# A state-space stage's W2 operand: transposed per batch on TensorE, or multiplied on VectorE from factors that were transposed once

## The chip, the cores and the metric

The kernel runs on one core of a Trainium2 chip. The metric is the device time of one execution in microseconds, the median of several runs. The engines are named as in the profile: PE is TensorE, PEld its weight load, DVE is VectorE, ACT is ScalarE, POOL is GpSimd, SP is SyncE, whose queue issues the DMAs. "L689" is line 689 of the kernel before; the changed kernel has other line numbers.

## The reference

A two-layer encoder trunk over 1024 frames of 1024 channels. Layer 0 projects its normalised input to `u`, gates, `q`, `k`, `v`; a diagonal complex state-space model works on `u` (64 groups of 16 channels, 64 states each), retention works on `q, k, v`; both are gated and projected back. Layer 1 is a gated convolution module. What matters here is the state-space model:

```python
lb = exp(a * dt)                          # complex, one per group g and state n
bb = ((lb - 1) / a)[..., None] * b        # complex, g x n x h (16 channels)
s[t] = lb * s[t - 1] + einsum('gnh,gh->gn', bb, u[t])
y[t] = real(einsum('ghn,gn->gh', c, s[t])) + d * u[t]
...
y = gelu(y); y = y * sigmoid(y @ glu_w + glu_b)
y_s5 = y * silu(g_s5)
```

The kernel takes eight frames at a time: the input of such a block to the state is a product with the table `W2[(j, h), n] = lb^j[n] * bb[n, h]`, j = 0 to 7.

## The kernel before, in words

Large products are made of three matmuls on a high and a low part of each operand (L146, L147, L148, 128x512). The front of layer 0 (`layer0_front`) first makes eight blocks of `u` (`u_block`), each stored to DRAM, and, between them, the parameters of the state-space model (`s5_params`): the powers of `lb` in `self.pr`, `self.pi` (state on the partitions) and the factors `bb` in `self.bbr`, `self.bbi`. GpSimd makes the latter last.

Then come 16 gate blocks (`gate_block`), two for each of eight batches B of the state-space model; a batch is eight groups. Each gate block is two halves of 24 matmuls in a PSUM tile `mm_g`, scaled on VectorE (L329) and sent through a SiLU on ScalarE (L330). Between the matmuls of the gate blocks stands the work of the batches:

- `s5_tables(B)`: GpSimd makes tables of 128x512 by outer products (`outer`, L642 to L644): Mr and Mi (powers times `bb`, state on the partitions), the rotations Tc and Ts, and W3. They have 18 instructions a batch in a fixed chain. ScalarE makes R8 (L671). The tables of batch B + 1 are made while batch B runs; Mr and Mi have one buffer and are freed by kp (below).
- `s5_states(B)`: loads U; PE transposes Mr and Mi, four 128x128 each (L689), ScalarE copies the results from PSUM to W2r and W2i (L691). PE multiplies W2 with U into the PSUM tiles V (L700). VectorE rotates V (L708 to L713), scans it (L715), rotates back (L722 to L725) and writes S (L726 to L728). PE also multiplies C with Mr and Mi to kp (L734, L735); ScalarE copies it to Kg, VectorE adds the diagonal (L738), PE transposes it (kt, L740), and it goes through DRAM (`k_d`, L744, L747) to become W1 (L749).
- `s5_out(B - 1)`: y = W1 x U + W3 x S on PE (L764, L770), copied by ScalarE, stored.

The order on each engine is decided when the kernel is built: a scheduler places the instructions by due times of its own, and each engine and SP's queue then run theirs strictly in that order. Tiles come from pools with a number of buffers per tag; a tile that takes a buffer waits until the last reader of the earlier one is done. PSUM has three banks for the gate blocks and five for everything else in this stage. After batch 7 the retention follows, then the rest of layer 0 and layer 1.

Of the kernel before, what the change touches and what calls it, by code (L numbers as in the profile page):

```python
# [11 lines left out]
F32 = mybir.dt.float32  # L12
# [3 lines left out]
ALU = mybir.AluOpType  # L16
# [3 lines left out]
P = 128  # L20
# [19 lines left out]
class Trunk:  # L40
# [167 lines left out]
    def layer0_front(self, st):  # L208
        tc, nc, A = self.tc, self.nc, self.A
# [30 lines left out]
        for kb in range(KB):  # L240
# [6 lines left out]
            t = xt[kb] = ev.tile([P, T], F32, name=f"x_{kb}", tag="xin", bufs=8)  # L247
            g = self.vec(V_NG0, kb)
            for h in range(2):
                c = slice(h * HALF, (h + 1) * HALF)  # L250
# [58 lines left out]
        def u_block(nb):  # L309
            ut = uv.tile([P, 8, P], F32, name=f"ut_{nb}", tag="ut", bufs=2)  # L310

            def evac(h, ps):
                r = self.R[:, h * HALF:(h + 1) * HALF]
                self.u_evac[nb] = nc.vector.tensor_tensor(
                    ut[:, ::-1, h * 64:(h + 1) * 64], ps[:].rearrange("p (m j) -> p j m", j=8),
                    r.rearrange("p (m j) -> p j m", j=8), op=ALU.mult)
            if nb < 2:
                for h in range(2):
                    evac(h, u01[nb][h])
            else:  # L320
                scaled(nb, self.wnext(f"u{nb}"), f"u{nb}", evac)
            nc.sync.dma_start(self.u_d[nb].rearrange("j h g m -> (h g) j m"), ut[:])
# [24 lines left out]
        for nb in range(5, 8):  # L347
            u_block(nb)
        self.s5_tab, self.s5_back, self.s5_last = {}, {}, None
        self.s5_tables(0)  # L350
        for nb in range(8, 24):
            B = (nb - 8) // 2
# [284 lines left out]
    def outer(self, B, o_r, o_i, ar, ai, br, bi, view, op_r=ALU.subtract, op_i=ALU.add):  # L637

        gp = self.nc.gpsimd
        for o, op, (a0, b0), (a1, b1) in ((o_r, op_r, (ar, br), (ai, bi)), (o_i, op_i, (ar, bi), (ai, br))):  # L640
# [2 lines left out]
            yield gp.tensor_tensor(view(o), a0, b0, op=ALU.mult)  # L643
            yield gp.tensor_tensor(o, o, t[:], op=op)  # L644

    def s5_tables(self, B):


        nc, w = self.nc, self.s5
        gp, v = nc.gpsimd, nc.vector  # L650
        qs = slice(4 * B, 4 * B + 4)

        Mr, Mi = self.big(f"Mr_{B}", "Mr", 1), self.big(f"Mi_{B}", "Mi", 1)
        vm = lambda ap: ap.rearrange("p q (j h) -> p q j h", j=8)
        bj = lambda t: t[:, qs, :].unsqueeze(2).broadcast_to([P, 4, 8, 16])
        pj = lambda t, o=0: t[:, o:o + 8, qs].rearrange("p j q -> p q j").unsqueeze(3).broadcast_to([P, 4, 8, 16])
        made = [self.outer(B, Mr[:], Mi[:], bj(self.bbr), bj(self.bbi), pj(self.pr), pj(self.pi), vm)]

        Tc, Ts = self.big(f"Tc_{B}", "Tc", 2), self.big(f"Ts_{B}", "Ts", 2)
        vt = lambda ap: ap.rearrange("p q (a b) -> p q a b", b=16)  # L660
        ea = lambda t: t[:, 0:8, qs].rearrange("p a q -> p q a").unsqueeze(3).broadcast_to([P, 4, 8, 16])
        eb = lambda t: t[:, 0:16, qs].rearrange("p b q -> p q b").unsqueeze(2).broadcast_to([P, 4, 8, 16])
        made.append(self.outer(B, Tc[:], Ts[:], ea(self.e2[0]), ea(self.e2[1]), eb(self.e1[0]), eb(self.e1[1]), vt))

        W3 = w.tile([P, 2, 4, P], F32, name=f"W3_{B}", tag="W3", bufs=2)
        made.append(self.outer(B, W3[:, 0], W3[:, 1], pj(self.pr, 1), pj(self.pi, 1), bj(self.cr), bj(self.nci), vm,
                               ALU.add, ALU.subtract))
        self.s5_last = self.chained(chain(*made), self.s5_last)
        R8 = self.big(f"R8_{B}", "R8", 2)
        for q in range(4):  # L670
            nc.scalar.mul(R8[:, q, :], self.m01[:], self.r8[:, 4 * B + q:4 * B + q + 1])  # L671
        self.s5_tab[B] = Mr, Mi, W3, Tc, Ts, R8

    def s5_states(self, B):
        nc, w = self.nc, self.s5
        gp, v = nc.gpsimd, nc.vector
        q0 = 4 * B
        Mr, Mi, W3, Tc, Ts, R8 = self.s5_tab.pop(B)


        U = w.tile([P, 8, P], F32, name=f"U_{B}", tag="U", bufs=2)
        nc.sync.dma_start(U[:], self.u_d[B].rearrange("j h g m -> (j h) g m"))


        W2 = []
        for nm, M in (("r", Mr), ("i", Mi)):
            ps = self.bank(f"w2{nm}_{B}")
            for q in range(4):
                nc.tensor.transpose(ps[:, q * P:(q + 1) * P], M[:, q, :], self.ident[:])  # L689
            t = self.big(f"W2{nm}_{B}", f"W2{nm}", 1)  # L690
            nc.scalar.copy(t[:].rearrange("p q n -> p (q n)"), ps[:])  # L691
            W2.append(t)

        V = []
        for c in range(2):
            ps = self.bank(f"v{c}_{B}")
            for q in range(4):
                for g2 in range(2):
                    r = slice(64 * g2, 64 * g2 + 64)
                    nc.tensor.matmul(ps[r, q * P:(q + 1) * P], W2[c][:, q, r], U[:, 2 * q + g2, :],  # L700
                                     start=True, stop=True)
            V.append(ps)
        fl = lambda t: t[:].rearrange("p q n -> p (q n)")

        tc, ts = fl(Tc), fl(Ts)
        vr, vi = V[0][:], V[1][:]
        t2, t4 = (fl(self.big(f"m{i}_{B}", "tmpV", 4)) for i in range(2))
        v.tensor_tensor(t2, vi, ts, op=ALU.mult)  # L708
        v.tensor_tensor(t4, vr, ts, op=ALU.mult)
        v.tensor_tensor(vr, vr, tc, op=ALU.mult)  # L710
        v.tensor_tensor(vi, vi, tc, op=ALU.mult)
        v.tensor_tensor(vr, vr, t2, op=ALU.add)
        v.tensor_tensor(vi, vi, t4, op=ALU.subtract)  # L713
        for z in (vr, vi):
            v.tensor_tensor_scan(z, fl(R8), z, 0.0, op0=ALU.mult, op1=ALU.add)  # L715

        S = w.tile([P, 2, 4, P], F32, name=f"S_{B}", tag="S", bufs=1)
        c1 = lambda t: t[:, :, 1:P]
        c0 = lambda t: t[:, :, 0:P - 1]
        zr, zi = (z.rearrange("p (q n) -> p q n", q=4) for z in (vr, vi))  # L720
        t2, t3 = (self.big(f"d{i}_{B}", "tmpV", 4) for i in range(2))
        v.tensor_tensor(c0(t2), c0(zi), c0(Ts), op=ALU.mult)  # L722
        v.tensor_tensor(c0(t3), c0(zr), c0(Ts), op=ALU.mult)
        v.tensor_tensor(c0(zr), c0(zr), c0(Tc), op=ALU.mult)
        v.tensor_tensor(c0(zi), c0(zi), c0(Tc), op=ALU.mult)  # L725
        v.tensor_tensor(c1(S[:, 0]), c0(zr), c0(t2), op=ALU.subtract)  # L726
        v.tensor_tensor(c1(S[:, 1]), c0(zi), c0(t3), op=ALU.add)
        v.memset(S[:].rearrange("p c q m -> p (c q) m")[:, :, 0:1], 0.0)  # L728


        kp = self.bank(f"kp_{B}")
        for q in range(4):
            o = kp[q * 32:(q + 1) * 32, :P]
            nc.tensor.matmul(o, self.cbr[:, q0 + q, :], Mr[:, q, :], start=True, stop=False)  # L734
            nc.tensor.matmul(o, self.cbni[:, q0 + q, :], Mi[:, q, :], start=False, stop=True)  # L735
        Kg = w.tile([P, P], F32, name=f"Kg_{B}", tag="Kg", bufs=1)
        nc.scalar.copy(Kg[:], kp[:, :P])
        v.tensor_tensor(Kg[:, :16], Kg[:, :16], self.dd[:, B, :], op=ALU.add)  # L738
        kp = self.bank(f"kt_{B}")
        nc.tensor.transpose(kp[:, :P], Kg[:], self.ident[:])  # L740
        Kt = w.tile([P, P], F32, name=f"Kt_{B}", tag="Kg", bufs=1)
        nc.scalar.copy(Kt[:], kp[:, :P])

        nc.sync.dma_start(self.k_d[B, 112:], Kt[:])  # L744
        Wd = w.tile([P, 8, P], F32, name=f"Wd_{B}", tag="yb", bufs=1)
        kd = self.k_d[B]
        nc.sync.dma_start(Wd[:], bass.AP(tensor=kd.tensor, offset=kd.offset, ap=[[P, P], [16 * P, 8], [1, P]]))  # L747
        W1 = w.tile([P, 8, P], F32, name=f"W1_{B}", tag="W1", bufs=2)
        nc.scalar.copy(W1[:].rearrange("p g (i h) -> p i g h", i=8), Wd[:].rearrange("p i (g h) -> p i g h", g=8))  # L749
        self.s5_back[B] = U, W1, W3, S  # L750

    def s5_out(self, B):


        nc = self.nc
        U, W1, W3, S = self.s5_back.pop(B)
        yb = self.s5.tile([P, 8, P], F32, name=f"yb_{B}", tag="yb", bufs=1)
# [3 lines left out]
        def products():  # L761
            for q in range(4):
                for g2 in range(2):
                    yield nc.tensor.matmul(ps[g2][:, cols(q)], W1[:, 2 * q + g2, :], U[:, 2 * q + g2, :],  # L764
                                           start=q == 0, stop=False)
# [727 lines left out]
```

## Time and profile before

| | |
|---|---|
| median of 3 runs | 1215.66 us (1213.5, 1215.66, 1219.05) |
| profiled execution | 1212.99 us, span 1211.2 us |
| granted TensorE clock, mean | 0.997 |
| PE busy | 1195.8 us, 99% |
| DVE, ACT, POOL busy | 748.2, 479.9, 664.0 us |
| eight batches of the state-space model | 101.3 to 333.6 us of the span |
| transposes of Mr and Mi (L689) | 64 |
| copies to W2r and W2i (L691) | 16, 0.58 us each |
| DMA | 226 MB on SP's queue, 55% of 16 engines |

Matmuls are pipelined: one that takes 0.39 us starts 0.23 us after the one before, so the cost of PE work is read from the distance of starts, not from durations. An engine's busy time is spread over stages with different limits; a stage is read from its own window.

### The profile page before, as it was taken

What the parts mean: (1) busy time and instruction counts of PE and PEld (TensorE: products, weight loads), DVE (VectorE), ACT (ScalarE), POOL (GpSimd) and SP (SyncE); (2) the same over time, 40 slices, a digit from 0 to 9 for tenths busy, and PEclk for the clock granted to TensorE, in tenths of its full rate; (3) what the DMA queues carried; (4) which work ended last, traced back from release to release, by engine and by line L of the source; (5) the groups of instructions that cost most, each with busy time, mean ns of one, the idle gap of its engine ahead of it and who ended that gap; (6) DMA issues with size and microseconds to landing.
All of it is one profiled execution on the core that took longest, in us unless ns stands there. A gap on an engine that the chain in (4) does not pass through costs nothing.

```text
span 1211.2 us, 17238 instructions
## 1 busy us (share of the span) xinstructions
PE 1195.8 (99%) x6468; PEld 1001.7 (83%) x6468; DVE 748.2 (62%) x1337; ACT 479.9 (40%) x706; POOL 664.0 (55%) x457
## 2 busy tenths in 40 slices
PE   9999999999999999999999999999999999999997
PEld 7888888888888889998888888888888788888876
DVE  7965655555412457457547102699999699899533
ACT  7212232332223233144335322545535575434652
POOL 2059988888237253253453651678453567758642
PEclk9999999999999999999999999999999999999998
DMA  9342433333385166467446877765667654356664
GB/s 334 105 140 72 140 129 132 128 128 139 110 284 177 53 208 160 155 208 256 143 158 223 285 272 250 243 209 208 212 241 256 222 192 152 123 176 240 237 254 149
DMA packets 100227, 227.11 MB, mean 188 GB/s; under 512 B 9264, under 2 KB 38192, under 8 KB 99504
## 3 DMA queue, kind: packets, MB, share of 16 engines
q1 hardware_dynamic: 100144, 226.01, 55.1%
q8 instruction: 51, 0.84, 0.3%
q14 instruction: 32, 0.26, 0.1%
HBM read 160.51 MB, written 61.28 MB: 183 GB/s over the span
## 4 chain that ended last, share of the span: by engine, by line
PE 94%; DMA 2%; ACT 2%; DVE 1%; issue 0%; SPq 0%; POOL 0%; DVEq 0%
PE mm_g L148 7%; PE mm_g L147 7%; PE mm_g L146 7%; PE mm_wo L148 5%; PE mm_wo L146 5%; PE mm_wo L147 5%; PE mm_a L148 2%; PE mm_b L147 2%; PE mm_b L148 2%; PE mm_a L146 2%; PE mm_a L147 2%; PE mm_b L146 2%; PE mm_u L148 2%; PE mm_u L147 2%; PE mm_u L146 2%; PE mm_glu L146 2%
## 5 line engine op out<-in xcount | busy, mean ns | idle before, releaser
L1194 DVE SCALAR_TENSOR_TENSOR cv<-u,convw,cv 128x512 f32<-128x512 f32 x398 | 273.5, 752 | 11.9 <-ACT cv L1180 9.6
L1174 POOL TENSOR_TENSOR tp<-tp,tp 128x512 f32<-128x512 f32 x64 | 82.9, 1296 | 45.5 <-ACT tp L1173 44.4
L148 PE MATMUL mm_g<-xh,wl_g 128*128 128x512 f32 x256 | 100.8, 394 | 0.0
L147 PE MATMUL mm_g<-xl,wh_g 128*128 128x512 f32 x256 | 100.6, 393 | 0.0
L146 PE MATMUL mm_g<-xh,wh_g 128*128 128x512 f32 x256 | 100.5, 393 | 0.0
L1173 ACT ACTIVATE tp<-u,convw 128x512 f32<-128x512 f32 x64 | 45.7, 719 | 35.6 <-POOL tp L1174 33.9
L329 DVE TENSOR_TENSOR gt<-mm_g,R 128x512 f32<-128x512 f32 x32 | 21.9, 686 | 60.0 <-PE mm_g L148 60.0
L138 POOL TENSOR_TENSOR wl_v<-wf_v,wh_v 128x1024 fp32r<-128x1024 f32 x12 | 29.0, 2425 | 51.9 <-ACT wh_v L137 51.9
L147 PEld LDWEIGHTS mm_g<-xl,wh_g 128*128 128x128 f32 x256 | 48.1, 188 | 11.3 <-issue 1.6
L148 PEld LDWEIGHTS mm_g<-xh,wl_g 128*128 128x128 f32 x256 | 48.0, 188 | 10.6
L146 PEld LDWEIGHTS mm_g<-xh,wh_g 128*128 128x128 f32 x256 | 48.1, 188 | 9.6
L148 PE MATMUL mm_oc<-zh,wl_woc 128*128 128x512 f32 (+1 forms) x152 | 54.3, 360 | 1.0 <-DMA wl_woc<-lo_woc 1.0
L1094 DVE TENSOR_TENSOR x<-mm_wo,xr 128x512 f32<-128x512 f32 x16 | 11.1, 691 | 70.3 <-PE mm_wo L148 39.6
L147 PE MATMUL mm_oc<-zl,wh_woc 128*128 128x512 f32 (+1 forms) x152 | 53.9, 357 | 0.6 <-POOL zl L1019 0.6
L146 PE MATMUL mm_oc<-zh,wh_woc 128*128 128x512 f32 (+1 forms) x152 | 54.3, 363 | 0.0
L1066 POOL TENSOR_TENSOR yg<-yg,yn 128x512 f32<-128x512 f32 x16 | 22.5, 1404 | 53.5 <-DMA yg<-gs_d 15.6
L148 PE MATMUL mm_a<-h1h,wl_ca 128*128 128x512 f32 x128 | 50.3, 393 | 1.1 <-DMA wl_ca<-lo_ca 1.1
L147 PE MATMUL mm_u<-xl,wh_u 128*128 128x512 f32 x128 | 50.1, 391 | 1.0 <-DVE xl L261 1.0
L146 PE MATMUL mm_g<-h1h,wh_cg 128*128 128x512 f32 x128 | 50.4, 394 | 0.0
L146 PE MATMUL mm_glu<-yh,wh_glu 128*128 128x512 f32 x128 | 50.3, 393 | 0.0
L146 PE MATMUL mm_b<-h1h,wh_cb 128*128 128x512 f32 x128 | 50.2, 392 | 0.0
L146 PE MATMUL mm_wo<-yrh,wh_wor 128*128 128x512 f32 x128 | 50.2, 392 | 0.0
(400 smaller groups left out, 3624.3 us busy)
## 6 DMA issues: line engine op xcount, KB each, us to landing
wf_g<-w_ab SPq DMA_DIRECT2D x16, 512.0 KB, 4.0
wf_wos<-w_out SPq DMA_DIRECT2D x16, 512.0 KB, 5.5
wf_wor<-w_out SPq DMA_DIRECT2D x16, 512.0 KB, 5.8
wf_cb<-w_c SPq DMA_DIRECT2D x16, 512.0 KB, 4.5
wf_ca<-w_c SPq DMA_DIRECT2D x16, 512.0 KB, 4.7
wf_woc<-w_out_c SPq DMA_DIRECT2D x16, 512.0 KB, 5.2
wf_v<-w_v SPq DMA_DIRECT2D x12, 512.0 KB, 4.5
wf_cg<-w_c SPq DMA_DIRECT2D x11, 512.0 KB, 4.0
```

The lines of the kernel that those rows point to most:

```text
L138: lo[i].tensor_tensor(wl[:].rearrange(fl)[:, c], wf[:, c], h.bitcast(F32), op=ALU.subtract)
L146: nc.tensor.matmul(ps, wh[:, kb, :], xh, start=start, stop=False)
L147: nc.tensor.matmul(ps, wh[:, kb, :], xl, start=False, stop=False)
L148: self.last_mm = nc.tensor.matmul(ps, wl[:, kb, :], xh, start=False, stop=stop)
L329: nc.vector.tensor_tensor(gt[:, c], ps[:], self.R[:, c], op=ALU.mult)
L1066: gp.tensor_tensor(yg[:], yg[:], yn[:], op=ALU.mult)
L1094: v.tensor_tensor(t[:], ps[:], xt[:], op=ALU.add)
L1173: nc.scalar.mul(sk[:], u[:, k:k + HALF], cw[:, nb, k:k + 1])
L1174: gp.tensor_tensor(s0[:], s0[:], sk[:], op=ALU.add)
L1194: v.scalar_tensor_tensor(dst[:], *tap, accs_[i][:], op0=ALU.mult, op1=ALU.add)
```

## The change

The table W2 is a product of a factor that depends on (j, n) and one that depends on (h, n). Instead of transposing the finished product for each batch, the changed kernel transposes the two factors for all batches once, after the last `u` block: `s5_turned` brings `bbr` and `bbi` into channel order on ScalarE, transposes eight 128x128 tiles of these and four of the powers on PE, copies them from PSUM on ScalarE, and stores them to the DRAM tiles `pt_d` and `bt_d`. For batches 1 to 7, `s5_w2` loads the factors of a batch with four DMAs whose source repeats rows (the 8 powers to 16 partitions each, the 16 channels eight times), and VectorE makes W2r and W2i with four products, a difference and a sum. Batch 0 still transposes Mr and Mi. Mr and Mi are made as before, since kp needs them. The four loaded tables have one buffer each; R8 and W1 now have one instead of two.

```diff
         self.s5_tab, self.s5_back, self.s5_last = {}, {}, None
+        self.s5_turned()
         self.s5_tables(0)
...
+    def s5_turned(self):
+        nc = self.nc
+        self.pt_d = self.dram.tile([2, 2, P, P], F32, name="pt_d")
+        self.bt_d = self.dram.tile([2, 4, P, P], F32, name="bt_d")
+        fl = lambda t, a, n: t[:, a * n:(a + 1) * n, :].rearrange("p a b -> p (a b)")
+        order = [self.big(f"hq{c}", "tmpV", 4) for c in range(2)]
+        for o, t in zip(order, (self.bbr, self.bbi)):
+            nc.scalar.copy(o[:].rearrange("p a (h q) -> p (a h) q", h=4), t[:].rearrange("p q h -> p h q"))
+        for i, (dst, parts) in enumerate((
+                (self.pt_d[:].rearrange("c a r n -> r (c a) n"), [fl(t, a, 4) for t in (self.pr, self.pi) for a in range(2)]),
+                (self.bt_d[0].rearrange("a r n -> r a n"), [order[0][:, a, :] for a in range(4)]),
+                (self.bt_d[1].rearrange("a r n -> r a n"), [order[1][:, a, :] for a in range(4)]))):
+            ps = self.bank(f"turn{i}")
+            for a, src in enumerate(parts):
+                nc.tensor.transpose(ps[:, a * P:(a + 1) * P], src, self.ident[:])
+            t = self.big(f"turned{i}", "tmpV", 4)
+            nc.scalar.copy(t[:].rearrange("p q n -> p (q n)"), ps[:])
+            nc.sync.dma_start(dst, t[:])
+
+    def s5_w2(self, B):
+        nc, v = self.nc, self.nc.vector
+        (ptr, pti), (btr, bti) = ([self.big(f"{n}{c}_{B}", f"{n}{c}", 1) for c in "ri"] for n in ("PT", "BT"))
+        dp, db = self.pt_d, self.bt_d
+        for c, (pt, bt) in enumerate(((ptr, btr), (pti, bti))):
+            nc.sync.dma_start(pt[:].rearrange("p q n -> p (q n)"),
+                              bass.AP(tensor=dp.tensor, offset=dp.offset + (c * 2 * P + 4 * B) * P,
+                                      ap=[[32 * P, 8], [0, 16], [1, 4 * P]]))
+            nc.sync.dma_start(bt[:].rearrange("p q n -> p (q n)"), bass.AP(tensor=db.tensor, offset=db.offset + (c * 4 * P + 4 * B) * P,
+                                                ap=[[0, 8], [32 * P, 16], [1, 4 * P]]))
+        w2r, w2i = (self.big(f"W2{nm}_{B}", f"W2{nm}", 1) for nm in "ri")
+        v.tensor_tensor(w2r[:], ptr[:], btr[:], op=ALU.mult)
+        v.tensor_tensor(w2i[:], ptr[:], bti[:], op=ALU.mult)
+        v.tensor_tensor(ptr[:], pti[:], bti[:], op=ALU.mult)
+        v.tensor_tensor(pti[:], pti[:], btr[:], op=ALU.mult)
+        v.tensor_tensor(w2r[:], w2r[:], ptr[:], op=ALU.subtract)
+        v.tensor_tensor(w2i[:], w2i[:], pti[:], op=ALU.add)
+        return [w2r, w2i]
...
-        R8 = self.big(f"R8_{B}", "R8", 2)
+        R8 = self.big(f"R8_{B}", "R8", 1)
...
-        self.s5_tab[B] = Mr, Mi, W3, Tc, Ts, R8
+        self.s5_tab[B] = Mr, Mi, W3, Tc, Ts, R8, self.s5_w2(B) if B else None
...
-        W2 = []
-        for nm, M in (("r", Mr), ("i", Mi)):
+        first, W2 = W2 is None, W2 or []
+        for nm, M in (("r", Mr), ("i", Mi)) if first else ():
...
-        W1 = w.tile([P, 8, P], F32, name=f"W1_{B}", tag="W1", bufs=2)
+        W1 = w.tile([P, 8, P], F32, name=f"W1_{B}", tag="W1", bufs=1)
```

In the changed kernel's built order, V of a batch from 1 on stands on PE right where a pair of gate blocks ends, with kp behind it; kt stands alone 28 to 34 gate matmuls after kp, and y after the first gate block of the pair. The first two of the six VectorE instructions of W2 for batch B + 1 stand just ahead of Kg (L738) of batch B.

## The prediction

> **What bounds the kernel now.** I read the page first (busy times, chain of waits), then the windows of the eight batches, then the instructions around one batch in order of time.
>
> The busy times and the shares of the chain:
>
> ```profile
> PE 1195.8 (99%) x6468; PEld 1001.7 (83%) x6468; DVE 748.2 (62%) x1337; ACT 479.9 (40%) x706; POOL 664.0 (55%) x457
> PE 94%; DMA 2%; ACT 2%; DVE 1%; issue 0%; SPq 0%; POOL 0%; DVEq 0%
> ```
>
> TensorE (PE) is busy for 99% of the span and is 94% of the chain that ended last. A microsecond of PE work taken out is a microsecond of time, unless PE then waits. The windows of two whole batches (columns: bounds, length, then busy time of PE, PEld, DVE, ACT, POOL, the granted clock, the DMA share, GB/s):
>
> ```profile
> 186.00:215.50 29.50, 29.50 (x203) 24.68 (x202) 15.63 (x22) 9.09 (x18) 23.74 (x18) 1.00 0.35 124
> 215.50:245.00 29.50, 29.50 (x203) 24.67 (x202) 15.68 (x22) 9.09 (x18) 23.73 (x18) 1.00 0.36 127
> ```
>
> PE never stands in a batch; VectorE has 13.8 us to spare of 29.5, GpSimd 5.8, DMA is at 0.36 and the clock is full. Now PE's timeline where a batch begins (start, duration, engine, line):
>
> ```profile
> 155.98 0.39 PE L147 MATMUL mm_g<-xl,wh_g 128*128 128x512 f32 x1
> 156.21 0.39 PE L148 MATMUL mm_g<-xh,wl_g 128*128 128x512 f32 x1
> 156.44 0.60 PE L689 MATMUL w2r<-ident,Mr 128*128 128x128 f32 x4
> 156.87 0.60 PE L689 MATMUL w2i<-ident,Mi 128*128 128x128 f32 x4
> 157.23 0.48 PE L146 MATMUL mm_g<-xh,wh_g 128*128 128x512 f32 x1
> 157.55 0.40 PE L147 MATMUL mm_g<-xl,wh_g 128*128 128x512 f32 x1
> 157.78 0.40 PE L148 MATMUL mm_g<-xh,wl_g 128*128 128x512 f32 x1
> 158.02 0.39 PE L146 MATMUL mm_g<-xh,wh_g 128*128 128x512 f32 x1
> 158.24 0.39 PE L147 MATMUL mm_g<-xl,wh_g 128*128 128x512 f32 x1
> ```
>
> Starts count, since matmuls overlap: one gate matmul per 0.227 us. Between the starts at 156.21 and 158.24 lie 2.03 us; five matmuls alone are 1.13. So the eight transposes cost PE 0.90 us a batch: 0.79 for themselves, the rest a slower restart.
>
> **Removed.** Batches 1 to 7 lose these eight transposes: 7 x 0.90 = 6.3 us off PE. Their 14 PSUM copies on ScalarE (L691, 0.58 each, 8.1 us) go too; ScalarE is busy 9.1 of 29.5 us, so that is worth nothing.
>
> **Added to PE.** Twelve transposes once, next to the eight of batch 0: 12 x 0.79 / 8 = 1.2 us. They wait for bbr and bbi through two ScalarE copies. GpSimd ends bbi at 84.0 (a row of 2.27 us from 81.75), and PE arrives at 101.3: 17 us of cover. ScalarE waits in its queue for bbi, and behind it stands the cast of the first gate weight, due at 102: still 15 us early.
>
> **Moved on PE.** In the built order V of batch B stands right at the end of the previous pair of gate blocks, kp behind it, and the single transpose kt 33 gate matmuls later (34 in batch 0, 28 in batch 7), no longer with y. Alone it costs 0.15 (batch 0 of before: starts 116.09 to 117.60, less six matmuls); beside y it cost 0.11 (141.90 to 142.01): 7 x 0.04 = 0.3 us. There are three interruptions a batch before and after.
>
> **Sum on PE:** -6.3 + 1.2 + 0.3 = -4.8 us, a batch of 28.65 us. Everything else must now not hold PE.
>
> **VectorE.** Six products of 128x512 for each of batches 1 to 7, all operands in SBUF. Bounds: 0.60 us (pitch of L708 to L711) below; the nearest row with both inputs in SBUF is the weight split L138, 128x1024, 1.21 to 2.39, median 1.54. I take 1.0 each: half the median plus part of its waiting. VectorE's batch becomes 15.65 + 6.0 = 21.7 of 28.65. Two of the six (W2r, W2i) stand ahead of Kg (L738), on which PE's kt waits. From the start of a batch: gate scaling and weight split until 2.3, two products and four rotations 4.4, Kg 0.7, so 7.4; kt stands at V 1.9, kp 0.6 and 33 x 0.227, so 10.0. The margin is 2.6 us. W2 itself is ready in the middle of the previous pair, about 13 us early. Only in pair 0 is S finished near the pair's end (122.5 to 123.2 before, plus about 4 of products, against 128); V of batch 1 needs its bank back: 0 to 0.7 us, which I leave in the range.
>
> **GpSimd.** It has no new instruction, but it shares something with VectorE. The rows, a VectorE split and three GpSimd products, two of them the same operation:
>
> ```profile
> 157.48 1.36 DVE L138 TENSOR_TENSOR wl_g<-wf_g,wh_g 128x1024 fp32r<-128x1024 f32 x1 [0.16 <-ACT wh_g L137]
> 157.72 2.09 POOL L642 TENSOR_TENSOR o<-s_bbi,s_pi 128x512 f32<-128x512 f32 x1
> 133.20 1.10 POOL L642 TENSOR_TENSOR o<-s_bbi,s_pi 128x512 f32<-128x512 f32 x1
> 110.03 1.11 POOL L643 TENSOR_TENSOR Mr<-s_bbr,s_pr 128x512 f32<-128x512 f32 x1 [0.53 <-PE kp L735]
> 110.03 0.68 DVE L709 TENSOR_TENSOR m<-v,Ts 128x512 f32<-128x512 f32 x1
> POOL Mr L643 <- PE kp L735: 28.4, 7, 5.3
> ```
>
> Beside a split GpSimd's product takes 2.09 for 1.10; beside a rotation that reads PSUM (110.03) it is not slowed. A product half as wide should cost GpSimd 0.5, at most 1.0: 3 to 6 us a batch. Against that stand the waits in the last row, 5.3 in a steady batch, less the 0.86 by which the batch shortens: 4.4. At 3 it fits. At 6 the tables fall 1.6 a batch behind, 11 by the end; Tc and Ts are due 8 us after they are made, so only the last two batches would wait, 1 to 3 us in all.
>
> The Trainium skill, "SBUF — State Buffer", section "Who interferes with whom", says that a VectorE instruction with two SBUF inputs contends with GpSimd's reads, and that the one that comes second stands until the first has ended. The rows agree in both halves; by that rule six products cost GpSimd 3.6 us, which fits too, and each product may have to stand for a whole GpSimd instruction, which is the second rival.
>
> **DMAs on SP's queue.** Three stores and 28 loads of 256 KB, 0.35 us of issue each. A load waits until VectorE has read its only buffer; behind it stand Wd, a gate store, a weight load and U. Gate weights are split about a pair ahead and U lands 7 us before V, so a few microseconds there cost nothing. For batches 2 on, the loads have about 17 us; loads of that size take:
>
> ```profile
> yn<-yn_d SPq DMA_DIRECT2D x16, 256.0 KB, 3.0
> k_d<-zero SPq DMA_DIRECT2D x1, 448.0 KB, 10.0
> ```
>
> I take 4 (yf, 256 KB, 4.1). Batch 1 is tighter: copies until 104, stores landed by 107.5, then four loads; Kg must not start later than 117.9 (kt at 118.6), so with both products the last load may take some 8 us. At 10, two or three waits of 1 to 2 us return.
>
> The Trainium skill, "DMA: Bandwidth & Descriptors", section on why a DMA increments its semaphore by 16, says that a copy is spread over at most as many engines as divide the slowest dimension of both sides; these loads' source begins with 8, so half the engines carry them. No DMA in this trace shows it; by it the first rival would be likelier.
>
> W1 and R8 go to one buffer: W1's copy waits for y (ends 17.5 us into a pair), but its data Wd lands near 20 anyway; R8 is made after the scans, some 18 us before the next ones. Cost: nothing.
>
> **The rivals.** (1) The waits return the gain: PE stands at kt and V of batches 0 to 2, 1 to 3 us each, as first loads of 10 us or products of 1.9 us would make it. 4 to 8 us back: 1212 to 1219. For: batch 1's chain of store, load, product, Kg has one pair only; against: DMA share 0.36.
>
> (2) The other side: VectorE becomes the bound of this stage. If every product stands behind a GpSimd instruction and takes as long as the longest split, 2.39, a batch is 15.65 + 14.3 = 30.0 us, with 1.3 for the wait of S on y (a row of before) 31.3: 7 x (31.3 - 29.5) + 1.2 = +13.8, so 1227; without that wait 1218. It decides from 2.17 a product ((28.65 - 15.65) / 6), or 1.95 with the wait. For: GpSimd is 80% busy; against: the median split of double width takes 1.54.
>
> That transposes remain is excluded: the built order has L689's only for batch 0.
>
> **How the numbers follow.** The profiled execution took 1212.99 (span 1211.2): 1208.2. From the median of the runs, 1215.66, it is 1210.9. The three runs (1213.5, 1215.66, 1219.05) scatter upwards and the profiled one lies below them, so I predict 1209.5, between. Half a percent, 6.1 us, is about what a measurement tells from no change; 1209.5 is just there, so the forecast case (0.76) divides into 0.46 faster and 0.30 same. Rival 1 has 0.12 (0.07 same, 0.05 slower), rival 2 0.12, all slower. Faster 0.46, same 0.37, slower 0.17. Low end: 1208.2 less 0.3% of scatter, 1204.5; the high end takes in rival 1, 1219, and leaves rival 2 out.
>
> **What would show it.** Right: PE 1191 us busy, no wait at V, kt or y; a batch of 28.6 to 28.7; products at 0.7 to 1.2; GpSimd's wait for kp shrinking to 1 to 2 us a batch but not gone. Wrong: PE waiting for VectorE at kt (Kg late) or at V, products near 2 us, a batch above 29.

## The result and the profile after

The changed kernel takes 1222.79 us (median of 15 runs, 1219.31 to 1225.42), the kernel before 1217.53 us (median of 15 runs, 1212.81 to 1221.09): a ratio of 1.0041, 95% interval 1.0029 to 1.0054. It is slower by 5 us where 6 us of gain were forecast, and its time lies above the range. The profiled execution took 1222.43 us, its span is 1220.6.

The page of the changed kernel, busy times and the shares of the chain that ended last:

```profile
PE 1195.2 (98%) x6424; PEld 999.3 (82%) x6424; DVE 793.3 (65%) x1379; ACT 477.3 (39%) x697; POOL 675.2 (55%) x457
PE 82%; DMA 8%; DVE 4%; issue 2%; ACT 2%; POOL 1%; SPq 1%; DVEq 0%; POOLq 0%; ACTq 0%
```

PE has 44 matmuls fewer, as forecast, but its busy time hardly fell (1195.8 to 1195.2), and its share of the chain went from 94% to 82%. The places that it gave up are held by DMA and VectorE: PE now waits for somebody. Its waits in this stage (line waited at, releaser; us in total, times, longest):

```profile
PE v L742 <- DVE W2i L685: 3.5, 1, 3.5
PE kt L782 <- DVE Kg L780: 2.3, 2, 1.8
PE v L742 <- DMA U<-u_d: 2.0, 1, 2.0
```

Each occurs once or twice, not seven times. The windows show the same (columns as before: bounds, length, busy time of PE, PEld, DVE, ACT, POOL, clock, DMA share, GB/s). The first is pair 1, the second a later batch:

```profile
130.20:162.00 31.80, 27.85 (x178) 22.87 (x178) 29.56 (x37) 7.77 (x14) 30.20 (x21) 0.89 0.48 155
...
192.00:221.00 29.00, 29.00 (x196) 24.14 (x195) 21.70 (x28) 8.60 (x16) 25.24 (x20) 1.00 0.50 166
```

The later batch is as forecast: PE without a gap, VectorE 21.7 us. From V of one batch to V of the next the time is 28.64 us there, where the kernel before had 29.51. Pair 1 is not: PE stands 4 of 31.8 us, VectorE is busy 93%, and the clock is at 0.89. PE's timeline between these (start, duration; the wait in front of an instruction in brackets), lines of other matmuls left out:

```profile
120.86 0.33 PE L782 MATMUL kt<-ident,Kg 128*128 128x128 f32 x1 [1.84 <-DVE Kg L780]
...
130.23 1.09 PE L742 MATMUL v<-U,W2r 128*64 128x128 f32 x16
...
134.78 1.97 PE L742 MATMUL v<-U,W2i 128*64 128x128 f32 x16 [3.45 <-DVE W2i L685]
...
138.31 0.63 PE L147 MATMUL mm_g<-xl,wh_g 128*128 128x512 f32 x1
138.73 0.63 PE L148 MATMUL mm_g<-xh,wl_g 128*128 128x512 f32 x1
139.16 0.63 PE L146 MATMUL mm_g<-xh,wh_g 128*128 128x512 f32 x1
...
167.80 1.09 PE L742 MATMUL v<-U,W2r 128*64 128x128 f32 x16 [1.98 <-DMA U<-u_d]
```

Batch 0's kt, batch 1's V and batch 2's V wait. After the wait of 3.45 us the gate matmuls start 0.43 us apart instead of 0.23: the granted clock is 0.5 there for 6.83 us.

Now the account. It is taken over the stretch in which the change acts, from the start of the first `u` matmul to that of the first matmul for `k`: 330.57 us before, 336.35 after. Forecast was 4.8 less, so 10.6 us are to be explained. The waits are 1.84 + 0.50 + 3.45 + 1.98 = 7.77 us (0.50 at kt of batch 1). The clock costs half of the 6.83 us, less the 1.29 of it in which PE stood anyway: 2.77. Together 10.5.

VectorE's side of it, its W2 products and the addition to Kg (L780), for which kt waits:

```profile
116.38 1.35 DVE L680 TENSOR_TENSOR W2r<-PTr,BTr 128x512 f32<-128x512 f32 x1 [3.28 <-DMA BTr<-bt_d]
117.74 1.81 DVE L681 TENSOR_TENSOR W2i<-PTr,BTi 128x512 f32<-128x512 f32 x1
119.48 1.33 DVE L780 TENSOR_TENSOR Kg<-Kg,s_s_dd 128x16 f32<-128x16 f32 x1
...
133.13 1.50 DVE L685 TENSOR_TENSOR W2i<-W2i,PTi 128x512 f32<-128x512 f32 x1
```

VectorE stands 3.28 us for BTr, which SP's queue had issued at 108.53: 7.8 us for a load that was taken at 4. The last of the six then ends at 134.6, and V of batch 1 had been due at 131.3. Two theories fit this so far. The first: the loads of batch 1 come late, and all that follows is their echo. The second: VectorE could not have done batch 1 in time anyway.

### The profile page after: what moved, and what is told of

It is laid out like the page before. It is cut to its first block, busy times and chain, and to the rows that moved or that the text cites. A ratio compares the mean times of both kernels' runs of the same rounds, so it can differ in the third digit from the quotient of the medians.

```text
span 1220.6 us, 17262 instructions
## 1 busy us (share of the span) xinstructions
PE 1195.2 (98%) x6424; PEld 999.3 (82%) x6424; DVE 793.3 (65%) x1379; ACT 477.3 (39%) x697; POOL 675.2 (55%) x457
## 4 chain that ended last, share of the span: by engine, by line
PE 82%; DMA 8%; DVE 4%; issue 2%; ACT 2%; POOL 1%; SPq 1%; DVEq 0%; POOLq 0%; ACTq 0%
PE mm_g L146 6%; PE mm_g L148 6%; PE mm_g L147 6%; PE mm_wo L148 4%; PE mm_wo L146 4%; PE mm_wo L147 4%; PE mm_a L148 2%; PE mm_b L148 2%; PE mm_b L147 2%; PE mm_a L146 2%; PE mm_a L147 2%; PE mm_u L148 2%; PE mm_b L146 2%; PE mm_u L147 2%; PE mm_u L146 2%; PE mm_glu L146 2%
## 5 line engine op out<-in xcount | busy, mean ns | idle before, releaser
L148 PE MATMUL mm_wo<-yrh,wl_wor 128*128 128x512 f32 x128 | 50.0, 391 | 0.8 <-POOL wl_wor L138 0.8
```

The costliest lines, as they stand in the source:

```text
L148: self.last_mm = nc.tensor.matmul(ps, wl[:, kb, :], xh, start=False, stop=stop)
```

## The experiments

The stretch from `u` to `k` and the waits are from one profile each; ratios are to the kernel before, run on the same chip.

| kernel | `u` to `k`, us | V to V, first two, us | waits of PE in the stage, us | ratio (95%) |
|---|---|---|---|---|
| before | 330.57 | 25.58, 29.51 | none | 1 |
| the change | 336.35 | 21.71, 37.57 | kt 2.3, V 3.5, U 2.0 | 1.0041 (1.0029 to 1.0054) |
| batch 1 transposed | 332.36 | 25.58, 23.60 (then 34.06) | kt 3.2, U 0.3 | 1.0015 (0.9999 to 1.0032) |
| turned early | 332.44 | 19.67, 35.11 | kt 3.9, V 0.6 | 1.0034 (1.0017 to 1.0051) |
| sixteen groups | 336.32 | 20.25, 36.57 | V 3.8, U 2.1, kt 0.4 | 1.0075 (1.0046 to 1.0103) |
| V's wait filled | 336.97 | 24.41, 34.72 | kt 3.0, U 1.6 | 1.0040 (1.0020 to 1.0060) |
| V held back | 329.63 | 28.75, 28.59 | kt 1.8 | 0.9995 (0.9974 to 1.0015) |
| V held, turned early | 325.88 | 25.11, 28.60 | none | 0.9946 (0.9925 to 0.9967) |
| two products | 330.49 | 19.67, 32.33 | kt 1.9 | 0.9963 (0.9941 to 0.9985) |
| rows once | 332.28 | 19.67, 35.51 | V 2.1, U 1.6, kt 1.2 | one run |
| V held, rows once | 325.59 | 25.11, 28.60 | none | 0.9964 (0.9947 to 0.9982) |
| early, rows once | 331.56 | 19.67, 33.93 | kt 2.7, V 0.6 | one run |
| rows once, eight | 331.52 | 19.67, 34.01 | V 2.1, U 1.2 | one run |
| adjacent rows, repeated | 334.76 | 20.25, 36.77 | V 3.8, kt 1.8, V 0.9 (ScalarE) | one run |

From batch 3 on, V to V is 28.6 us in every kernel with the change. So the products never bind the steady stage; the whole loss of this stretch lies in the first pairs.

### First round: are the loads the cause?

The expectations of this round weigh the late tables of the first batch against the load that the products put on VectorE.

**Batch 1 transposed.** Batch 1 also takes its W2 from the transposes, so the loads have a pair more.

```diff
-        self.s5_tab[B] = Mr, Mi, W3, Tc, Ts, R8, self.s5_w2(B) if B else None
+        self.s5_tab[B] = Mr, Mi, W3, Tc, Ts, R8, self.s5_w2(B) if B > 1 else None
```

> Batch 1 keeps the transposes of before; batches 2 to 7 use the multiplied tables. Theory A (the loss is the start of the chain: tables of batch 1 stored, loaded and multiplied within one pair of gate blocks; 8 us of PE waits and 2.7 us of half clock, all before 168 us): none of these waits, six batches gain 0.90 each, less 1.2 and 0.3: 3.9 us faster than before, ratio 0.997, PE without a wait from 101 to 340 us, every batch from 2 on 28.65 us. Theory B (the loss is the standing load: six products on VectorE beside GpSimd, 28 loads on SP's queue, felt in the stage and after it): at most 1 us better than the changed kernel, ratio 1.003 to 1.005.

Measured: ratio 1.0015. The wait did not go; it moved one batch on, to kt of batch 2, though the loads had a pair more. VectorE waits for no load there; ahead of that Kg it stands for ScalarE's cast of a gate weight, after it had stood 0.77 us for PE:

```profile
PE kt L782 <- DVE Kg L780: 3.2, 1, 3.2
161.83 2.17 DVE L138 TENSOR_TENSOR wl_g<-wf_g,wh_g 128x1024 fp32r<-128x1024 f32 x1 [3.63 <-ACT wh_g L137]
```

The short interval moved with it: V to V is 25.58, then 23.60, with 74 gate matmuls in the second instead of 96.

**Turned early.** The turn stands ahead of the last `u` block, so the tables are in SBUF before batch 0 begins.

```diff
-        for nb in range(5, 8):
+        for nb in range(5, 7):
             u_block(nb)
...
         self.s5_turned()
+        u_block(7)
         self.s5_tables(0)
```

> The twelve transposes, their copies and stores stand one u block earlier (10.9 us); all else as in the changed kernel, seven batches multiplied. Theory A: the tables of batch 1 land about 10 us earlier, before VectorE comes to them; no wait at kt or V of batches 0 to 2, clock full: 4.8 us faster than before, ratio 0.996. Theory B: as the changed kernel, ratio 1.003 to 1.005.

Measured: ratio 1.0034. VectorE no longer waits for a load, and V comes almost on time. But kt of batch 1 waits:

```profile
129.88 1.09 PE L743 MATMUL v<-U,W2i 128*64 128x128 f32 x16 [0.60 <-DVE W2i L686]
143.13 0.33 PE L783 MATMUL kt<-ident,Kg 128*128 128x128 f32 x1 [3.86 <-DVE Kg L781]
```

So late loads alone are not the cause; they are a part of it (3.9 us in the stretch).

**Sixteen groups.** Batch 1's loads (and its loads of U and Wd) are written so that the slowest dimension of the source is 16 instead of 8.

```diff
-                                       ap=[[32 * P, 8], [0, 16], [1, 4 * P]]))
+                                       ap=[[0, 16], [32 * P, 8], [1, 4 * P]] if B == 1 else [[32 * P, 8], [0, 16], [1, 4 * P]]))
...
```

> Batch 1 alone has its rows in another order (h outside j), so that the source of its four table loads begins with 16 instead of 8; U of batch 1 and its W1 rows follow that order, W1's data then comes in eight small DMAs. If eight DMA engines were what made these loads slow (7.8 us from issue to VectorE's start, DMA share 0.5 at 120 to 180 GB/s), they land in 4 to 5 us at a share near 1, VectorE starts 3 us earlier, the wait at kt of batch 0 goes (1.8 us) and that at V of batch 1 shrinks from 3.5 to under 1: 4 to 7 us better than the changed kernel, ratio 0.998 to 1.001. If the loads are slow for another reason (rows read many times, the store before them), they land as late as before: ratio 1.004.

Measured: VectorE starts 7.4 us after BTr's issue (107.72 to 115.13), against 7.8. Almost nothing; and the waits stay. The ratio, 1.0075, is above that of the change, but the stretch is the same; where the rest comes from is open.

**V's wait filled.** Eighteen matmuls into an unused bank are chained between the halves of V of batch 1, so that PE does not stand there and the clock does not drop.

```diff
+            if B == 1 and c == 0:
+                idle = self.bank("filler", aux=False)
+                held = self.chained((nc.tensor.matmul(idle[:, :P], self.ones[:], self.ones[:], start=True, stop=True)
+                                     for _ in range(FILL)), mm)
...
```

> The changed kernel with 18 matmuls of ones (128x128, results unused) between the two halves of V of batch 1, where PE stood for 3.45 us. If the halved granted clock behind that wait is caused by it and costs what the starts show (2.7 us), PE runs on at full clock: 2 to 3 us better than the changed kernel, ratio 1.002. If the clock falls anyway, or costs nothing on the path: ratio 1.004 or above.

Measured: ratio 1.0040, no better. V's wait was filled, but BTr took 8.4 us in this profile, kt of batch 0 waited 3.0 us, and the clock fell behind that. So the run does not tell what the halved clock behind V's wait had cost.

### Second round: the place of V

The first round left this. Before, V of a batch stood behind 22 gate matmuls of its pair; in batch 1 these lie between the transposes and V:

```profile
127.36 0.60 PE L689 MATMUL w2i<-ident,Mi 128*128 128x128 f32 x4
...
132.92 1.09 PE L700 MATMUL v<-U,W2r 128*64 128x128 f32 x16
```

In the changed kernel it stands at the pair's very start, since nothing has to be transposed first. So in the first batch to be multiplied PE gives VectorE only 74 gate matmuls from V to V, 19.67 us if it never waits; from then on it is 96, 28.64 us. The advance is made once and gains nothing, since PE's work is the same. But VectorE is short once by the difference. This is theory C in the expectations.

**V held back.** V of batches 1 to 7, with the rest of `s5_states`, is built after the first half of the pair's gate block.

```diff
-            if nb % 2 == 0:
+            if nb == 8:
                 self.s5_states(B)
-            gate_block(nb, self.wnext(f"g{nb}"), self.gs_d if nb < 16 else self.gr_d)
+            gate_block(nb, self.wnext(f"g{nb}"), self.gs_d if nb < 16 else self.gr_d,
+                       (lambda: self.s5_states(B)) if nb % 2 == 0 and B else None)
```

(`gate_block` hands the last argument to `scaled`, which calls it after the first half.)

> The V and y block of batches 1 to 7 is built after the first half (24 matmuls) of its pair's first gate block, instead of at the pair's very start; everything else is as in the change. Theory C (the change moved V from 22 gate matmuls into its pair to the pair's start, so that the first multiplied batch has only 74 gate matmuls from V to V, about 19.6 us, while VectorE needs 22 us or more for it; the arrears are paid as waits at V, kt and U of the next batches, and as a halved clock behind them): no wait of over 1 us at V W2i or kt; what may be left is up to 2 us for U or the late first loads; gate stage 3 to 5 us shorter than the kernel before, ratio 0.995 to 0.998. Rival (the place of V does not matter, the late loads of batch 1's tables alone make the arrears): waits of 2 to 4 us at V or kt of batch 1 or 2 as in the change, ratio 1.002 to 1.004.

Measured: ratio 0.9995. The waits at V and U are gone, 6.7 us of the stretch. One is left, at kt of batch 0, for which BTr is too late as in the change:

```profile
121.25 0.33 PE L785 MATMUL kt<-ident,Kg 128*128 128x128 f32 x1 [1.84 <-DVE Kg L783]
```

**V held, turned early.** Both edits together.

> V held back as in e5_v_held, and the factors turned one u block earlier, as in e2_turn_early. Theory C: V to V of the first batch is about 28 us and the tables lie there 10 us ahead, so no wait of over 0.5 us at V, kt or y, no drop of the clock, the gate stage 4.8 us shorter than the kernel before; ratio 0.996. Rival (VectorE cannot pay for six products in pairs 0 and 1 wherever V stands): a wait of 2 us or more at kt or V of batch 1 or 2, ratio 1.000 to 1.003.

Measured: ratio 0.9946, and faster than both kernels. The page's busy times, and the window from V of batch 0 to V of batch 1, then from there to V of batch 2:

```profile
PE 1192.5 (99%) x6424; PEld 998.0 (82%) x6424; DVE 807.0 (67%) x1379; ACT 476.9 (39%) x697; POOL 675.9 (56%) x457
```

```profile
108.60:133.70 25.10, 25.10 (x148) 20.51 (x147) 22.37 (x27) 8.05 (x14) 22.72 (x17) 1.00 0.34 114
133.70:162.30 28.60, 28.60 (x194) 23.86 (x193) 24.39 (x29) 8.22 (x16) 28.05 (x21) 1.00 0.50 165
```

PE has no gap. VectorE does 22.37 us of work in the first interval: more than the 19.67 us that the place of V in the changed kernel leaves it. The stretch is 325.88 us, 4.69 less than before; the forecast's sum was 4.8.

**Two products.** Turned early, V at the pair's start, but of the six VectorE instructions of W2 only two products and a multiplication of an eighth of the width are made; the second half of each sum is left out.

```diff
-        v.tensor_tensor(ptr[:], pti[:], bti[:], op=ALU.mult)
-        v.tensor_tensor(pti[:], pti[:], btr[:], op=ALU.mult)
-        v.tensor_tensor(w2r[:], w2r[:], ptr[:], op=ALU.subtract)
-        v.tensor_tensor(w2i[:], w2i[:], pti[:], op=ALU.add)
+        v.tensor_tensor(w2i[:, :, 0:16], pti[:, :, 0:16], btr[:, :, 0:16], op=ALU.mult)
```

> The factors turned one u block earlier, V at the pair's start as in the change, but four of the six VectorE products of each batch left out, so that the second half of each sum in W2 is missing (one small multiplication stays, that the tables are still read). VectorE loses about 4 to 6 us a batch. Theory C (arrears of VectorE in the first batch): kt of batch 1 no longer waits 3.9 us but under 1, no drop of the clock behind it, ratio 0.996 to 0.998. Rival (the loads, or ACT's cast ahead of Kg, hold kt): kt of batch 1 still waits 2 us or more, ratio 1.001 to 1.003.

Measured: ratio 0.9963, but kt of batch 1 still waits 1.86 us, between what the two theories gave. Four products less halved the wait (3.86). The rest is not VectorE's products. VectorE had no arrears left in front of that Kg: it stood for PE, and then for ScalarE's cast of a gate weight:

```profile
129.03 0.69 DVE L329 TENSOR_TENSOR gt<-mm_g,R 128x512 f32<-128x512 f32 x1 [2.25 <-PE mm_g L148]
132.29 2.09 DVE L138 TENSOR_TENSOR wl_g<-wf_g,wh_g 128x1024 fp32r<-128x1024 f32 x1 [2.56 <-ACT wh_g L137]
```

The cast stood in ScalarE's queue behind the copy to W1, which waited for Wd until 130.26. In "turned early" the same cast held VectorE 2.35 us, so that at most 1.5 of the 3.86 us are its products there. In "V held, turned early" it held VectorE 1.34 us, and no wait of PE followed. So the short interval is short for two: for VectorE, which in the changed kernel does not pause from 116.38 until W2i is ready, and for the way of W1 through DRAM and ScalarE's queue, which alone makes the wait in this run and in "batch 1 transposed".

### Third round: why the loads are slow

**Rows once.** The loads read 128 different rows of 2 KB, next to each other, so the tables hold other values.

```diff
-                                       ap=[[32 * P, 8], [0, 16], [1, 4 * P]]))
+                                       ap=[[4 * P, P], [1, 4 * P]]))
...
-                                                ap=[[0, 8], [32 * P, 16], [1, 4 * P]]))
+                                                ap=[[4 * P, P], [1, 4 * P]]))
```

> The change, but the four table loads of a batch read 128 different rows of 2 KB each, instead of 8 or 16 rows repeated, so that the tables' contents are other ones. If reading the same rows again and again is what made batch 1's BTr land 7.8 us after its issue, it lands within 4 us here, VectorE's first product starts 3 us or more earlier than at 116.4 us, and V of batch 1 waits under 1 us. If the store of the factors, the weight block and four loads sharing the queues made it, BTr takes 7 us again and V waits 3 us or more.

Measured: the loads of batch 1 land in 2.5 to 4.3 us (issues in a window of that kernel; KB each, us to landing), BTr a little above the 4 expected, and VectorE starts at 112.55, not 116.38:

```profile
PTr<-pt_d SPq DMA_DIRECT2D x1, 256.0 KB, 4.0
PTi<-pt_d SPq DMA_DIRECT2D x1, 256.0 KB, 4.2
BTr<-bt_d SPq DMA_DIRECT2D x1, 256.0 KB, 4.3
BTi<-bt_d SPq DMA_DIRECT2D x1, 256.0 KB, 2.5
```

V comes after 19.67 us, but its second half waits 2.1 us all the same, as theory C has it; the expectation's "under 1 us" was wrong, since it took the loads for the only cause.

**V held, rows once.** V held back, the turn at the change's place, and 128 different rows. This separates what was left in "V held back".

> V held back as in e5_v_held, the factors turned at the place of the change, and the loads reading 128 different rows as in e8_rows_once (so the tables' contents are other ones). Theory C with the slow loads as its second cause: kt of batch 0, which waited 1.84 us in e5_v_held, waits under 0.5 us, no other wait, no drop of the clock in the gate stage, from the first u matmul to the first k matmul 326 us (the change 336.35, e5_v_held 329.63, e6_held_early 325.88); ratio 0.993 to 0.997. Rival (the turn's place so close to batch 0 costs by itself, by the copies and stores): kt of batch 0 still waits 1 us or more, 328 us or more.

Measured: 325.59 us, no wait of PE in the stage, ratio 0.9964. Quick loads do what the early turn does.

**Early, rows once.**

> The factors turned one u block earlier as in e2_turn_early, V at the pair's start, and the loads of 128 different rows (so the tables' contents are other ones). Theory C: with the tables there early the loads no longer matter, and VectorE's arrears of the first batch stay: kt of batch 1 waits 2.5 us or more, as in e2_turn_early (3.86 us), first u to first k matmul 331 to 333 us. Rival (the loads made the arrears there too): the wait is under 1 us and the stretch 326 to 329 us.

Measured: kt of batch 1 still waits 2.7 us, 331.56 us. With the tables there early, quicker loads do not take away the arrears.

**Rows once, eight**, and **adjacent rows, repeated**: 128 different rows in eight groups of sixteen; and 8 (or 16) rows that lie side by side, read 16 (or 8) times.

```diff
 rows once, eight
+                                       ap=[[64 * P, 8], [4 * P, 16], [1, 4 * P]]))
 adjacent rows, repeated
+                                       ap=[[4 * P, 8], [0, 16], [1, 4 * P]]))
+                                                ap=[[0, 8], [4 * P, 16], [1, 4 * P]]))
```

> e8_rows_once with the same 128 different rows written as 8 groups of 16, so that the slowest dimension of the source is 8 as in the change (the tables' contents are other ones). If the repeated rows made batch 1's loads slow, they land in 3 to 4.5 us as in e8_rows_once and VectorE starts its first product by 113.5 us. If the eight groups did, BTr takes 7 us again and VectorE starts at 115 us or later.

> The change, its loads repeating rows as before (8 rows 16 times, 16 rows 8 times), but these rows lie next to each other in DRAM instead of 16 KB apart (the tables' contents are other ones). If reading a few rows again and again is what makes the loads slow, VectorE's first product starts at 115.5 us or later and V of batch 1 waits 2.5 us or more for W2i, as in the change. If it is the distance of the rows, it starts by 113.5 us, as in e8_rows_once and e11_rows_once_eight.

Measured: with eight groups of different rows BTr lands 4.4 us after its issue and VectorE starts at 113.37, within the bound. With repeated rows side by side it starts at 115.27, a little before the bound of the expectation, and still waits for the load, which took 6.6 us from its issue at 108.62; V waits 3.75 us:

```profile
115.27 1.11 DVE L680 TENSOR_TENSOR W2r<-PTr,BTr 128x512 f32<-128x512 f32 x1 [2.17 <-DMA BTr<-bt_d]
```

What differs between these loads is seen while they run (columns as before: the changed kernel, then sixteen groups, then eight groups of different rows):

```profile
111.00:114.00 3.00, 3.00 (x17) 2.49 (x14) 2.10 (x4) 1.55 (x2) 2.71 (x3) 1.00 0.51 165
110.50:113.50 3.00, 3.00 (x28) 2.34 (x21) 2.44 (x4) 1.55 (x2) 2.38 (x3) 1.00 0.66 167
109.00:112.00 3.00, 3.00 (x51) 2.54 (x52) 1.03 (x2) 0.41 (x2) 1.17 (x2) 1.00 1.05 366
```

In the changed kernel the DMA share is 0.51, at 165 GB/s. The trace's semaphore records fit half of the engines: each of its table loads posts 9 times, once 1 us after the issue and eight times 3 us after it or later, where the other DMAs post 16 times. Sixteen groups post 16 times, and so do the eight groups of different rows, which lie end to end. So that last run does not test eight engines; sixteen groups does. There BTr was still slow (7.4 us) and the rate still 167 GB/s, though more of the engines were busy. By this one profile the larger part is that the same rows are read again and again. Their distance has a smaller share (6.6 against 7.8 us, both on eight engines, one profile each), and the number of engines the smallest (7.4 against 7.8).

## Why the prediction was wrong, step by step

- **The sum on PE was right.** -4.8 us forecast, -4.69 measured once nothing waits; a batch of 28.65 us forecast, 28.64 measured in the changed kernel itself.
- **VectorE's load was right.** 21.7 us a batch forecast and measured. The six take 0.68, 0.68, 0.67, 0.90, 1.90 and 1.49 us (medians), 6.3 for a forecast of 6.0. In batch 1 alone they took 8.2. The second rival did not happen.
- **The step that failed: "W2 itself is ready in the middle of the previous pair, about 13 us early".** It holds in the steady batches (11.7 us). For batch 1 it was not 13 but -3.45 us. The prediction saw that V moves to the end of the previous pair, and costed the move on PE (0.3 us). It did not work out what the move does to the batch in which it is made: VectorE loses 22 gate matmuls, 5 us, from that interval, just when its work grows by 8. Apart from the loads, pair 0 was looked at only for S and for V's bank, "0 to 0.7 us". Held back, V's place alone gives 6.7 of the 10.6 us.
- **The loads of batch 1 were mis-sized.** Taken at 4 us within rows of 3.0 to 10.0, with 8 named as the limit; BTr took 7.8 and Kg started at 119.48 instead of 117.9. A load of 7.8 us was within that limit, but the limit had the loads issued at 107.5 and a product at 1.0; BTr was issued at 108.53, and the two products took 1.35 and 1.81. The late loads are worth 3.9 us (turned early). The two parts add up: 6.7 + 3.9 = 10.6, and both together give 10.5.
- **"U lands 7 us before V, so a few microseconds there cost nothing" was wrong in batch 2.** SP's queue stood before the next load of BTi until VectorE's L682 had read the last one, up to 8.5 us, and then for those of BTr and PTr in the same way. What stood behind them came late: Wd was issued at 157.73, U at 159.39, and V waited 1.98 us. That wait of SP's queue over the kernel (total, times, longest):

```profile
SPq L677 <- DVE PTr L682: 40.8, 6, 8.5
```

- **The first rival's waits are what happened**, with a chance of 0.12 and too small a price: 4 to 8 us back, where 10.5 came back. The waits at kt and V of batches 0 to 2 were right (7.8 us); the halved clock behind them (2.8) had no place in the sum. Its cause, slow first loads or slow products, is the smaller part; the place of V is not in it.
- **The Trainium skill.** "DMA: Bandwidth & Descriptors", section on why a DMA increments its semaphore by 16, would have the loads slow because their source begins with 8. That eight engines carry them agrees with the trace (DMA share 0.51 and 9 posts, above). That this makes them late is not borne out: with sixteen groups of repeated rows on all engines BTr took 7.4 us for 7.8. "SBUF — State Buffer", section "Who interferes with whom", would explain why the last two of the six take 1.49 and 1.90 us where the first three take 0.68. The trace agrees. Of the 42 VectorE instructions of W2 in the changed kernel 32 start while a GpSimd instruction runs; each of them ends 0.54 to 0.61 us after that instruction's end, after 0.68 to 1.91 us in all. The other ten take 0.67 to 0.69. One of the 32:

```profile
151.46 1.82 POOL L644 TENSOR_TENSOR Ts<-s_e2r,s_e1i 128x512 f32<-128x512 f32 x1
151.97 1.87 DVE L684 TENSOR_TENSOR W2r<-W2r,PTr 128x512 f32<-128x512 f32 x1
```

So what each of the six costs depends on where it falls in GpSimd's chain, which is why batch 1's six took 8.2 us. GpSimd's cost came out smaller than both estimates: 24.88 us busy in 28.64 against 23.73 in 29.50, 1.2 us a batch for 3 to 6.

Of the 9.4 us between the two profiled spans, 5.8 are in the stretch. Another 2.7 lie in the retention that follows, from the first matmul for `k` to the first of the GLU, which takes 215.9 us in the profile before and 216.7 to 222.9 in those of the thirteen changed kernels, with waits of 0 to 4.5 us for VectorE's rotated q. The profile before is of an execution below the median of its kernel. Whether the change has a hand in this stage was not settled; it does not alter its instructions.

## What to carry to other kernels

When a change frees an instruction to move ahead, look for the one interval that becomes shorter by the move, and put the other engines' work of that interval beside it; a steady batch does not show it. An advance on the engine that is full buys nothing by itself, so put the freed instruction back where it stood: here the same edit went from 1.0041 to 0.9946 by that and by an earlier turn. Where a wait of PE cannot be avoided, count the clock behind it too.

## What the runs showed of the hardware that was not expected

**Loads that repeat their source rows are slow.** BTr of batch 1, 256 KB from 16 rows of 2 KB, each read 8 times, beside three loads like it: VectorE, which waited for it, started 6.6 to 8.4 us after its issue. From 128 different rows it landed in 4.3 to 4.5 us. While these loads ran, the DMAs moved 165 to 174 GB/s with repeated rows, on eight engines as on sixteen, and 366 to 376 with different rows, other traffic included.

**The clock halves after about half a window of standing.** In the records of the granted clock, every stretch at 0.5, apart from the one at a kernel's end, is 3.41 us long, or two of these, and the distances between them are whole multiples of 3.413 us (with sixteen groups: 9 and 88). Laid on that grid, a window at full speed in which PE stood 1.84 us or more was followed by one at half speed (V held back: 1.84 at kt); one with 1.81 was not (the changed kernel's wait for U), nor were four others of 1.54 to 1.61. One window does not fit: in "adjacent rows, repeated", late in the kernel (674.2), 1.54 us in three pieces were followed by half speed. So the standing that the records show does not draw the line alone. In a window already at half speed 1.29 us were enough to keep it there. The same wait of 1.84 us at kt of batch 0 cost nothing more in the changed kernel, where it fell across two windows, 0.81 and 1.03. The Trainium skill, "TensorE: Matmul & The Clock Gate", section on the clock gate, states a free-running window of 3413 ns, and the records agree; its section on the oscillation speaks of idle gaps over about 3.4 us, and here little more than half of that was enough.
